# Stick attention two key blocks at a time, projections of 384 columns, and tile 6's expert lists during the last queries

## The chip, the core and the metric

The kernel runs on one core of a Trainium2 chip, in one launch. The metric is the device time of that launch in microseconds. The core's engines are TensorE (PE; its weight loads stand apart as PEld), VectorE (DVE), ScalarE (ACT), GpSimd (POOL) and SyncE (SP), beside 16 DMA engines. Engines run their own queues in order and wait for each other through semaphores.

## The reference

One decoder block on 1024 tokens of width 1024, all in 32-bit floats. A normalised input feeds three token mixers; their results are gated, summed, projected and added to x. Then every token chooses 8 x 16 of 16384 experts.

```python
h = rms_norm(x, g_mix)
# A: stick-breaking attention, 8 heads of 64, strictly causal
z = q k^T * 64**-0.5
log_keep = where(past, log_sigmoid(-z), 0)
between = reverse_cumsum(log_keep) - log_keep
a = where(past, exp(log_sigmoid(z) + between), 0);  y_sb = a v
# B: 12 heads of 64 in 3 groups, window 128 keys at stride 1, 4, 16, rms_norm on q and k, merged by lse
# C: 4 heads of 128 over 256 memory tokens, rms_norm on q and k, softmax
x = x + (sum of sigmoid(h W_gate + b) * (y_* W_o)) W_out
h2 = rms_norm(x, g_ffn)
sc = (h2 w_q) . subkeys                 # 8 heads x 2 halves x 128 scores a token
s1, i1 = top_k(sc[0], 16); s2, i2 = top_k(sc[1], 16)
top_s, pos = top_k(s1[:, None] + s2[None, :], 16);  gate = softmax(top_s)
out = x + sum over 8 x 16 of gate * gelu(u[idx] . h2) * v[idx]
```

## The kernel before

Tokens lie in 8 tiles of 128, taken in three groups: tiles 0 and 1, then 2 to 4, then 5 to 7 (`GROUPS = (2, 3, 3)`; below: the first, second and third group). `phase1` takes a group through stages: `stick_breaking` (four pairs of heads), `dilated` with the pieces of `memory_attn` set in between, `gating`, `out_proj`, `ffn_norm`, and `select`, the queries and scores of the experts. The keys and values of the first two groups are kept in DRAM for the later ones.

Matmul operands are in 32-bit floats: a product shows as two PE records. A projection `proj_T` works with at most 256 columns (`SUB = 2` tiles), so a group of three tiles is taken as 256 + 128 columns, each with its own PSUM bank (tile name `bank`, four buffers) and, for normalised q and k, its own chain in `head_norm` and `rstd_rows`: ScalarE squares, a product with ones, VectorE's ms, ScalarE's Ln, Exp and Square, and three or four VectorE passes. `Pipe` delays each piece's later parts by one tick, so that they stand behind the next piece's first products.

In `stick_part` a round takes one key block b against one or two query tiles: scores z in a bank, Abs, Exp and Ln on ScalarE (tile `e`), sp on VectorE, and one tick later (part1) the product with `ntri` (the sum inside the block) and with `nones` over S (the sum of later blocks), Exp, and S += sp; another tick later (part2) the product with v. A double tile works on 2 heads x 256 columns, the third tile of a group alone on 2 x 128.

Six tiles have their experts gathered: for every step, 128 rows of u and 128 of v come by one indirect DMA each, issued by GpSimd (L1030); VectorE multiplies u with h2 and sums (L1092, two passes a step), Gelu on ScalarE once in four steps, and TensorE sums v by weights (L1116; pb at L1083 spreads h2). There are 768 steps. Tiles 4 and 6 (`DENSE`) are computed against all experts instead: `gate_matrix` turns their lists into a matrix (tiles `ab`, products into g, stored to gd), and `dense` streams u and v once (L1134), adding up in acc (L1264).

The lists come from VectorE: `top16` (L819 to L823) for 16 halves, `pairs` and another `top16` for 8 heads. For a group's first tile they are made in `select` (the part `first`); for the others in `topk`, which is a side job, in the order 1st, 3rd, 2nd tile.

What stands beside what is decided in the main loop: a step is issued, then `fill` takes pieces of the rest (phase 1, gate matrix, dense) by the planner's costs, until a due time.

```python
            due = max(due + LEAST, pe - LEAST)
            while filler[0] is not None and (dma > pe or pe < due):
                a, b = fill(1)
```

What is left of the steps when the rest is done runs alone at the end (the tail). A scheduler then orders each engine's queue; ScalarE keeps the program's order.

Of the kernel before, what the change touches and what calls it, by code (L numbers as in the profile page):

```python
# [17 lines left out]
D = 1024  # L18
# [28 lines left out]
SUB = 2  # L47
# [29 lines left out]
def block_kernel(ctx: ExitStack, tc: tile.TileContext, io):  # L77
# [239 lines left out]
    def rstd_rows(ssq, n, dim):  # L317

        y = tmp.tile([128, NS], F32, name="rs")
        ms = tmp.tile([128, NS], F32, name="ms")  # L320
        nc.vector.tensor_scalar(ms[:, :n], ssq, 1.0 / dim, EPS, op0=OP.mult, op1=OP.add)
        actf(y[:, :n], ssq, AF.Ln, scale=1.0 / dim, bias=eps)
        actf(y[:, :n], y[:, :n], AF.Exp, scale=-0.5)
        a = tmp.tile([128, NS], F32, name="sq")
        actf(a[:, :n], y[:, :n], AF.Square)
        nc.vector.scalar_tensor_tensor(a[:, :n], a[:, :n], -0.5, ms[:, :n], op0=OP.mult, op1=OP.mult)
        nc.vector.scalar_tensor_tensor(y[:, :n], a[:, :n], 1.5, y[:, :n], op0=OP.add, op1=OP.mult)
        return y

    def norm_T(xT, n, gain, out):  # L330

        ps_ = []
        for c0 in range(0, n, NS):
            w = min(NS, n - c0)
            p = bank()
            for k in range(KD):
                sq = tmp.tile([128, NS], F32, name="sq")
                actf(sq[:, :w], xT[:, k, c0:c0 + w], AF.Square)
                mm(p[:, :w], ones, sq[:, :w], start=k == 0, stop=k == KD - 1)
            ps_.append((c0, w, p))  # L340
        yield
        for c0, w, p in ps_:
            y = rstd_rows(p[:, :w], w, D)
            for k in range(KD):
                nc.vector.scalar_tensor_tensor(out[:, k, c0:c0 + w], xT[:, k, c0:c0 + w], gain[:, k:k + 1],
                                               y[:, :w], op0=OP.mult, op1=OP.mult)
        yield

    def proj_T(w, h, n, c0=0):

        p = bank()
        if type(w) is tuple:
            wh, wl = w
            for k in range(KD):
                hh, hl = (x[:, k % 4, c0:c0 + n] for x in h[1][k // 4])
# [4 lines left out]
        for piece, o, m in pieces(h[0], c0, n):  # L360
# [4 lines left out]
    def pieces(h, c0, n):  # L365

        if type(h) is not list:
            return [(h[:, :, c0:c0 + n], 0, n)]
# [12 lines left out]
    def head_norm(p, n, dim, lhs, done):  # L381

        sq = tmp.tile([128, NS], F32, name="sq")
# [41 lines left out]
    def stick_breaking(pipe, weights, hT, n0, G, oT):  # L425
        N = G * 128
        t0 = n0 * 128
        for p in range(4):
# [7 lines left out]
            w = weights("w_in", p)  # L436
            for i, g in subs(G):
                pq = proj_T(w, hT, g * 128, i * 128)
                for s in range(2):
                    r = slice(64 * s, 64 * s + 64)  # L440
                    nc.vector.tensor_scalar(q[r, s, i * 128:(i + g) * 128], pq[r, :g * 128], 0.125, None, op0=OP.mult)
                pipe.tick()
                yield
            w = weights("w_in", 4 + p)
            for i, g in subs(G):
                pk = proj_T(w, hT, g * 128, i * 128)
                actf(kT[:, t0 + i * 128:t0 + (i + g) * 128], pk[:, :g * 128], AF.Copy)
                pipe.tick()
                yield
# [10 lines left out]
    def stick_part(pipe, p, kT, v, q, n0, G, out):  # L460
# [49 lines left out]
    def dilated(pipe, weights, hT, n0, G, oT, between):  # L510
        N = G * 128
        t0 = n0 * 128
        for pp in range(2):
            ks, vs, b0s = [], [], []
            for g, (dil, nb) in enumerate(DIL):
# [18 lines left out]
                wq = weights("w_in", NB_SB + pr)  # L534
                for i0, m in subs(G):
                    c = slice(i0 * 128, (i0 + m) * 128)
                    pq = proj_T(wq, hT, m * 128, i0 * 128)

                    def done_q(y, pq=pq, g=g, c=c, m=m * 128):
                        for s in range(2):  # L540
                            r = slice(64 * s, 64 * s + 64)
                            nc.vector.scalar_tensor_tensor(qpad[r, 2 * g + s, c], pq[r, :m], gs[r, 0:1],
                                                           y[r, :m], op0=OP.mult, op1=OP.mult)
                    part = head_norm(pq, m * 128, 64, ones64, done_q)
                    pipe.tick()
                    pipe.push(part)
                    yield
                wk = weights("w_in", NB_SB + 6 + pr)
                for i0, m in subs(G):
                    c = slice(w0 + i0 * 128, w0 + (i0 + m) * 128)  # L550
                    pk = proj_T(wk, hT, m * 128, i0 * 128)

                    def done_k(y, pk=pk, k=k, w0=w0, pr=pr, c=c, m=m * 128, last=i0 + m == G):
                        nc.vector.scalar_tensor_tensor(k[:, c], pk[:, :m], gk_dil, y[:, :m],
                                                       op0=OP.mult, op1=OP.mult)
                        if last and n0 + G < NT:
                            nc.scalar.dma_start(c_dk[pr, :, t0:t0 + N], k[:, w0:w0 + N])
# [830 lines left out]
```

## Time and profile before

| | |
|---|---|
| three runs | 4009.22, 4027.1 (median), 4034.66 us |
| profiled execution | 4013.32 us, span 4011.5 us, mean granted TensorE clock 0.905 |
| busy | PE 3361.7, DVE 2632.8, POOL 1506.7, ACT 1256.0 us |
| moved | 1186.65 MB, mean 296 GB/s |
| first step at | 506.9 us |
| last dense addition | 3930 us |

Busy time is the union of an engine's instructions. PEclk is the TensorE clock that was granted, as a share of full speed. "DMA share" is the mean busy share of the 16 DMA engines. In a row of a timeline stand the start, the time, the engine, the line, the operation and the tiles (out<-in), and in brackets the idle time before it with what ended it. In a row of waits stand who waited for whom, the total, the times and the longest. In a row of groups: the count, the busy time, the mean in ns, and the idle time before.

### The profile page before, as it was taken

The page shows a single profiled execution, that of the slowest core. Times are in us where ns is not written, and L with a number is a line of the kernel's source. Part 1 is how long each engine was busy: PE and PEld are TensorE (multiplying, and loading weights), DVE is VectorE, ACT ScalarE, POOL GpSimd, SP SyncE. Part 2 cuts the span into 40 slices and gives each one's busy share as a digit, 9 for nine tenths or more (in the row PEclk, how much of TensorE's full clock was granted, in tenths as well). Part 3 has the DMA queues.
Part 4 walks back from the last instruction along what each step waited for, and adds up shares of the span by engine and source line. Part 5 has one row for each costly group of instructions (what it writes and reads, how often), then busy time and mean ns, then how long its engine had stood idle before and what let it go on. Part 6 is the DMA issues. An engine that isn't in the chain of part 4 may idle for free.

```text
span 4011.5 us, 65667 instructions
## 1 busy us (share of the span) xinstructions
PE 3361.7 (84%) x24130; PEld 2529.9 (63%) x24130; DVE 2632.8 (66%) x8339; ACT 1256.0 (31%) x2637; POOL 1506.7 (38%) x1544
## 2 busy tenths in 40 slices
PE   7999788878799888878878999793366999999995
PEld 6889666656555676655756556681134888878772
DVE  5443885455434557876555466469886888888885
ACT  4442343433300113544434211110023444433340
POOL 0000043433345443444434344355552343333335
PEclk9999888988899998998989999895587999999996
DMA  4345487877699997787877799897998899999989
GB/s 148 110 129 176 152 306 245 293 268 264 234 330 385 374 352 285 268 280 257 317 254 270 268 381 379 331 364 278 353 329 313 331 375 356 364 359 360 348 307 340
DMA packets 347034, 1186.65 MB, mean 296 GB/s; under 512 B 38808, under 2 KB 80792, under 8 KB 327256
## 3 DMA queue, kind: packets, MB, share of 16 engines
q0 software_dynamic: 221184, 805.40, 54.9%
q1 hardware_dynamic: 102960, 338.34, 23.3%
q10 hardware_dynamic: 22568, 38.70, 2.6%
q8 instruction: 191, 3.13, 0.3%
q14 instruction: 131, 1.07, 0.1%
HBM read 1142.58 MB, written 39.71 MB: 295 GB/s over the span
## 4 chain that ended last, share of the span: by engine, by line
PE 62%; DVE 16%; issue 6%; DMA 5%; another core or an unknown queue 5%; ACT 5%; POOL 1%; ACTq 1%; SPq 0%; DVEq 0%; POOLq 0%
PE bank L116 34%; PE bank L1134 18%; PE po L1116 7%; DVE u L1092 5%; ACT e L127 2%; DMA u<-in_u,iT 1%; PE pb L1083 1%; DMA gd<-g 1%; PE bank L120 1%; ACT L125 1%; DMA v<-in_v,iT 1%; DVE ab L1159 1%; DVE ul L1219 1%; POOL v L1030 1%
## 5 line engine op out<-in xcount | busy, mean ns | idle before, releaser
L1030 POOL DMA_INDIRECT u<-in_u,iT x768 | 759.5, 989 | 1778.2 <-DVE u L1092 757.5
L1092 DVE SCALAR_TENSOR_TENSOR u<-u,pb 128x512 f32<-128x512 f32 x1536 | 1009.2, 680 | 216.9 <-PE pb L1083 105.3
L1030 POOL DMA_INDIRECT v<-in_v,iT x768 | 746.4, 972 | 716.5 <-PE po L1116 490.6
L116 PE MATMUL bank<-wide,w 128*128 128x128 f32 (+2 forms) x2304 | 554.9, 397 | 34.3 <-ACT S L127 16.0
L1116 PE MATMUL po<-v,wz 128*32 128x256 f32 x6144 | 466.7, 416 | 85.6 <-DVE wz L1105 34.0
L116 PEld LDWEIGHTS bank<-wide,w 128*128 128x128 f32 x2304 | 396.8, 201 | 179.5 <-issue 21.9
L1116 PEld LDWEIGHTS po<-v,wz 128*32 128x32 f32 x6144 | 187.5, 115 | 318.1 <-issue 109.0
L1134 PE MATMUL bank<-hh,uh 128*128 128x256 f32 x1024 | 293.4, 286 | 32.2 <-issue 31.8
L116 PE MATMUL bank<-w,wide 128*128 128x128 f32 x2304 | 279.4, 280 | 29.2 <-issue 15.7
L1134 PE MATMUL bank<-hh,ul 128*128 128x256 f32 x1024 | 293.2, 286 | 5.8 <-DVE ul L1219 5.0
L116 PEld LDWEIGHTS bank<-w,wide 128*128 128x128 f32 x2304 | 269.2, 195 | 45.4 <-issue 24.8
L1134 PE MATMUL bank<-hl,uh 128*128 128x256 f32 x1024 | 291.1, 284 | 0.0
L127 ACT ACTIVATE e<-bank 128x256 f32<-128x256 f32 (+2 forms) x256 | 117.2, 458 | 502.0 <-PE bank L116 202.3
L1083 PE MATMUL pb<-b,which 96*128 96x512 bf16 x384 | 141.3, 419 | 102.6 <-DVE u L1092 83.1
L1134 PEld LDWEIGHTS bank<-hh,uh 128*128 128x128 f32 x1024 | 197.8, 193 | 38.7 <-issue 34.6
L1134 PE MATMUL bank<-vh,wh 128*128 128x512 f32 x512 | 212.2, 419 | 7.8 <-ACT wh L127 5.7
L1134 PEld LDWEIGHTS bank<-hh,ul 128*128 128x128 f32 x1024 | 197.6, 193 | 15.2 <-issue 7.3
L1134 PE MATMUL bank<-vl,wh 128*128 128x512 f32 x512 | 200.7, 392 | 0.0
L1134 PE MATMUL bank<-vh,wl 128*128 128x512 f32 x512 | 198.5, 392 | 0.6 <-DVE wl L1251 0.6
L1134 PEld LDWEIGHTS bank<-hl,uh 128*128 128x128 f32 x1024 | 197.7, 193 | 0.4 <-issue 0.4
L1264 DVE TENSOR_TENSOR acc<-acc,bank 128x512 f32<-128x512 f32 x256 | 168.8, 685 | 37.2 <-PE bank L1134 31.7
L116 PE MATMUL bank<-big,w 128*128 128x128 f32 (+1 forms) x1024 | 182.6, 335 | 3.1 <-issue 3.1
(259 smaller groups left out, 6117.1 us busy)
## 6 DMA issues: line engine op xcount, KB each, us to landing
vr<-in_vd SPq DMA_DIRECT2D x64, 1024.0 KB
ur<-in_uT SPq DMA_DIRECT2D x64, 1024.0 KB
w<-in_w_in SPq DMA_DIRECT2D x102, 512.0 KB
w<-in_w_gate SPq DMA_DIRECT2D x72, 512.0 KB
w<-in_w_pq SPq DMA_DIRECT2D x48, 512.0 KB
g<-gd SPq DMA_DIRECT2D x16, 1024.0 KB
w<-in_w_o SPq DMA_DIRECT2D x48, 256.0 KB
w<-in_w_out SPq DMA_DIRECT2D x24, 512.0 KB
```

Of the source, the lines that this page charges most:

```text
L116: nc.tensor.matmul(out, lhsT, rhs, **kw)
L120: nc.tensor.transpose(out, in_, ident)
L125: nc.scalar.preload_act_table_set(s)
L127: nc.scalar.activation(out, in_, f, **kw)
L1030: nc.gpsimd.indirect_dma_start(out=t, out_offset=None, in_=io[kind], in_offset=bass.IndirectOffsetOnAxis(ap=ap, axis=0))
L1083: nc.tensor.matmul(pb, which[:, jj].rearrange("p q s -> p (q s)"), box["b3"][:, hh * 512:(hh + 1) * 512], start=True, stop=True)
L1092: nc.vector.scalar_tensor_tensor(u[:, f], u[:, f], 1.0, pb, op0=OP.mult, op1=OP.mult, accum_out=self.parts[:, hh, i:i + 1])
L1116: nc.tensor.matmul(po[32 * k:32 * k + 32, h:h + 256], wz[:, i, :], v[:, 256 * k:256 * k + 256], start=jj == 0 and i == 0, stop=jj == QB - ...
L1134: nc.tensor.matmul(out, lhsT, rhs, **kw)
L1159: nc.vector.tensor_scalar(ab[:, 0, :], iota, sl[:, 0, t:t + 1], sl[:, 2, t:t + 1], op0=OP.is_equal, op1=OP.mult)
L1219: nc.vector.tensor_sub(lo, r[:, x], hi)
L1264: nc.vector.tensor_add(acc[:, i, f], acc[:, i, f], o)
```

## The change

1. `stick_single` takes a single tile two key blocks at a time: z, e and sp hold 2 blocks x 2 heads x 128. The nearer block's sum is added to the farther one by a product of its own (`nones`, sp). 
2. `proj_T` takes all of a group's columns (384) into one bank; q, k and memory queries have one norm chain for the group. `rstd_rows` scales the sum in the bank, and Ln reads it there. `memory_attn` works by head, with the parts of both sub-tiles in one step.
3. In the third group `select` makes the lists of tiles 5 and 6; tile 6's lie in three tiles of `ab`. `topk` runs in the order 1st, 2nd, 3rd tile.
4. `dense` loads and splits its first operands ahead of the wait for the gate matrix.

```diff
     def rstd_rows(ssq, n, dim):
-        nc.vector.tensor_scalar(ms[:, :n], ssq, 1.0 / dim, EPS, op0=OP.mult, op1=OP.add)
-        actf(y[:, :n], ssq, AF.Ln, scale=1.0 / dim, bias=eps)
+        nc.vector.tensor_scalar(ssq, ssq, 1.0 / dim, EPS, op0=OP.mult, op1=OP.add)
+        actf(y[:, :n], ssq, AF.Ln)
...
             for i, g in subs(G):
-                yield from stick_part(pipe, p, kT, v, q[:, :, i * 128:(i + g) * 128], n0 + i, g,
-                                      oT[:, p, i * 128:(i + g) * 128])
+                args = pipe, kT, v, q[:, :, i * 128:(i + g) * 128], n0 + i, oT[:, p, i * 128:(i + g) * 128]
+                yield from stick_single(*args) if g == 1 else stick_part(*args[:5], g, args[5])
+    def stick_single(pipe, kT, v, q, n, out):
+        S = tmp.tile([128, 2, NS], F32, name="S", bufs=1)[:, :, :128]
+        for b in range(n, -1, -2):
+            bs = [b, b - 1][:b + 1]
+            m = len(bs)
+            z = bank().rearrange("p (x s n) -> p x s n", x=2, s=2)
+            for x, y in enumerate(bs):
+                for s in range(2):
+                    mm(z[:, x, s], kT[:, y * 128:(y + 1) * 128], q[:, s], start=x == 0 and s == 0, stop=False,
+                       skip_group_check=True)
...
+            actf(e[:, :m], z[:, :m], AF.Abs)
+            actf(e[:, :m], e[:, :m], AF.Exp, scale=-1.0)
+            actf(e[:, :m], e[:, :m], AF.Ln, bias=1.0)
+            nc.vector.scalar_tensor_tensor(sp[:, :m], z[:, :m], 0.0, e[:, :m], op0=OP.max, op1=OP.add)
+            def part1(b=b, m=m, z=z, e=e, sp=sp):
+                for x in range(m):
+                    mm(z[:, x], ntri, sp[:, x], start=False, stop=False, skip_group_check=True)
+                    if b < n:
+                        mm(z[:, x], nones, S, start=False, stop=False, skip_group_check=True)
+                if m == 2:
+                    mm(z[:, 1], nones, sp[:, 0], start=False, stop=True, skip_group_check=True)
+                actf(e[:, :m], z[:, :m], AF.Exp)
...
-                wq = weights("w_in", NB_SB + pr)
-                for i0, m in subs(G):
-                    pq = proj_T(wq, hT, m * 128, i0 * 128)
-                    part = head_norm(pq, m * 128, 64, ones64, done_q)
+                pq = proj_T(weights("w_in", NB_SB + pr), hT, N)
+                part = head_norm(pq, N, 64, ones64, done_q)
...
-            for _ in range(2 * len(subs(G))):
+            for _ in range(2):
                 next(between)
...
         scs = [wide.tile([128, 8 * NMAX], F32, name="wide")[:, :2048].rearrange("p (a b) -> p a b", a=16)
-               if i == SUB else sc.tile([128, 16, 128], F32, name="sc") for i in range(G)]
+               if G > SUB and i == 1 else sc.tile([128, 16, 128], F32, name="sc") for i in range(G)]
+        lists = [new_lists()]
+        if n0 + G == NT:
+            a, b, c = (gm.tile([128, 2, 128], F32, name="ab") for _ in range(3))
...
             def first(hp=hp):
-                top16(s16[:, h, hp % 2, :], i16[:, h, hp % 2, :], scs[0][:, hp, :])
+                for l, x in zip(lists, scs):
+                    half_list(hp, x, *l)
...
-        for i in (0, 2, 1)[:G] if G > SUB else range(G):
+        for i in range(G):
...
         while len(stored) < ND:
             cost[0] += 1500
             yield
-        while next(gates) < ND:
-            cost[0] += 800
-            yield
         hh = dp.tile([128, KD, TD], F32R, name="hh", bufs=1)
...
         us[0] = split(ur[0], 0, "u", 2)
+        while next(gates) < ND:
+            cost[0] += 800
+            yield
```

Three places in the built order show what moves; line numbers of the changed kernel differ by up to 45. First TensorE, in the stick attention of tile 7 (single): before, two rounds of one key block, with a step's products (po) between them. e,big is the product with v, qpad,big the scores of a later block.

```order
L116 MATMUL bank<-e,big 64x128 x2
L116 MATMUL bank<-sp,ntri 128x128
L116 MATMUL bank<-S,none 128x128
L116 MATMUL bank<-sp,ntri 128x128
L116 MATMUL bank<-S,none 128x128
L1116 MATMUL po<-v,wz 32x256 x11
L116 MATMUL bank<-qpad,big 128x128 x2
L116 MATMUL bank<-e,big 64x128 x2
L116 MATMUL bank<-sp,ntri 128x128
L116 MATMUL bank<-S,none 128x128
```

In the changed order the same place holds one round of two blocks:

```order
L116 MATMUL bank<-qpad,big 128x128 x4
L116 MATMUL bank<-e,big 64x128 x4
L116 MATMUL bank<-sp,ntri 128x256
L116 MATMUL bank<-S,none 128x256
L116 MATMUL bank<-sp,ntri 128x256
L116 MATMUL bank<-S,none 128x256
L116 MATMUL bank<-sp,none 128x256
```

Products are twice as wide, with one more (sp,none), and TensorE meets ScalarE's e and VectorE's sp once where it met them twice.

Second VectorE, in the third group's last queries: before, the list of tile 5 alone (scores in sc, values in s, the 8 heads' merges in ts and pos).

```order
L819 MAX ts<-sc 128x8
L819 MAX s_20802<-sc 128x8
L820 MAX_INDEX pos<-ts,sc 128x8
L820 MAX_INDEX i_20803<-s_20802,sc 128x8
L821 MATCH_REPLACE sc<-ts,sc 128x112
L821 MATCH_REPLACE sc<-s_20802,sc 128x128
```

In the changed order tile 6's (scores in wide, lists in ab) stands beside it:

```order
L859 MAX s_19472<-sc 128x8
L859 MAX ab<-wide 128x8
L860 MAX_INDEX i_19473<-s_19472,sc 128x8
L860 MAX_INDEX ab<-ab,wide 128x8
L861 MATCH_REPLACE sc<-s_19472,sc 128x128
L861 MATCH_REPLACE wide<-ab,wide 128x128
L862 MAX s_19472<-sc 128x8
L862 MAX ab<-wide 128x8
L863 MAX_INDEX i_19473<-s_19472,sc 128x8
L863 MAX_INDEX ab<-ab,wide 128x8
L1137 SCALAR_TENSOR_TENSOR u,parts<-u,pb 128x512 x4
```

Each score row of the queries now brings ten passes where it brought five, ahead of the steps' products (the last row).

Third SyncE's loads at the start of dense: sl is tile 6's list for the gate matrix, g the finished matrix, ur and vr the experts' rows. Before:

```order
L1149 DMA sl<-seld 128x384
L1008 DMA b_24146<-b3d 96x1024
L1077 DMA row<-xres 32x256 x4
L247 DMA g<-gd 128x8x256 x2
L247 DMA ur<-in_uT 128x2048 x3
```

In the changed order:

```order
L247 DMA ur<-in_uT 128x2048
L1194 DMA sl<-seld 128x384
L247 DMA ur<-in_uT 128x2048
L247 DMA vr<-in_vd 128x2048 x2
L1053 DMA b_23144<-b3d 96x1024
L1122 DMA row<-xres 32x256 x4
L247 DMA g<-gd 128x8x256 x2
```

The first u rows move from behind g to ahead of sl. By the counts of steps (rows of L1092, in the changed kernel L1137, on VectorE), 601.5 steps stand ahead of the first dense addition before and 556.5 now, and behind the last one 28 before and 70 now.

More of the change, by code (lines that the diff above doesn't have):

```diff
@@ L330, in norm_T, with proj_T @@
     def norm_T(xT, n, gain, out):
[L332 to L340, printed above, removed]
-        yield
[L342 to L346, printed above, removed]
+        p = bank()
+        for k in range(KD):
+            sq = tmp.tile([128, NMAX], F32, name="sq")
+            actf(sq[:, :n], xT[:, k, :n], AF.Square)
+            mm(p[:, :n], ones, sq[:, :n], start=k == 0, stop=k == KD - 1)
+        yield
+        y = rstd_rows(p[:, :n], n, D)
+        for k in range(KD):
+            nc.vector.scalar_tensor_tensor(out[:, k, :n], xT[:, k, :n], gain[:, k:k + 1], y[:, :n],
+                                           op0=OP.mult, op1=OP.mult)
         yield
-    def proj_T(w, h, n, c0=0):
+    def proj_T(w, h, n):
         p = bank()
@@ L548, in dilated @@
[L548 to L557, printed above, removed]
-                    part = head_norm(pk, m * 128, 64, ones64, done_k)
-                    pipe.tick()
-                    pipe.push(part)
-                    yield
+                pq = proj_T(weights("w_in", NB_SB + pr), hT, N)
@@ new lines, in done_q @@
+                def done_q(y, pq=pq, g=g):
+                    for s in range(2):
+                        r = slice(64 * s, 64 * s + 64)
+                        nc.vector.scalar_tensor_tensor(qpad[r, 2 * g + s, :N], pq[r, :N], gs[r, 0:1],
+                                                       y[r, :N], op0=OP.mult, op1=OP.mult)
+                part = head_norm(pq, N, 64, ones64, done_q)
+                pipe.tick()
+                pipe.push(part)
+                yield
+                pk = proj_T(weights("w_in", NB_SB + 6 + pr), hT, N)
@@ new lines, in done_k @@
+                def done_k(y, pk=pk, k=k, w0=w0, pr=pr):
+                    nc.vector.scalar_tensor_tensor(k[:, w0:w0 + N], pk[:, :N], gk_dil, y[:, :N],
+                                                   op0=OP.mult, op1=OP.mult)
+                    if n0 + G < NT:
+                        nc.scalar.dma_start(c_dk[pr, :, t0:t0 + N], k[:, w0:w0 + N])
+                part = head_norm(pk, N, 64, ones64, done_k)
+                pipe.tick()
+                pipe.push(part)
+                yield
@@ L730, in back @@
             actf(oT[:, 6 + h, i0 * 128:i0 * 128 + N], pt[:, :N], AF.Copy)
-        part = head_norm(pq, N, 128, ones, done)
-        pipe.tick()
-        pipe.push(part, scores, mix, mix2, back)
+        return box, scores, mix, mix2, back
     def gating(pipe, weights, hT, N, oT, mT):
@@ L859, in select, with new_lists, half_list @@
         pipe.flush()
[L860 removed]
+        side.append(topk(n0, G, scs, out, lists))
+    def new_lists():
+        return (tk.tile([128, 8, 2, 16], F32, name="s16", bufs=2), tk.tile([128, 8, 2, 16], U32, name="i16"),
+                tk.tile([128, 8, 16], F32, name="ts"), tk.tile([128, 8, 16], U32, name="pos"))
+    def half_list(hp, scores, s16, i16, ts, pos):
+        h = hp // 2
+        top16(s16[:, h, hp % 2, :], i16[:, h, hp % 2, :], scores[:, hp, :])
+        if hp % 2:
+            cand = candidates(scores)
+            pairs(cand, s16, h)
+            top16(ts[:, h, :], pos[:, h, :], cand[:, h, :])
     def candidates(sc):
```

141 lines of the change are left out of this document (73 added, 68 removed).

## The prediction

> **What bounds the kernel now.** I read the page first: which engine the chain that ended last runs through.
>
> ```profile
> PE 3361.7 (84%) x24130; PEld 2529.9 (63%) x24130; DVE 2632.8 (66%) x8339; ACT 1256.0 (31%) x2637; POOL 1506.7 (38%) x1544
> PE 62%; DVE 16%; issue 6%; DMA 5%; another core or an unknown queue 5%; ACT 5%; POOL 1%; ACTq 1%; SPq 0%; DVEq 0%; POOLq 0%
> ```
>
> TensorE carries 62% of the chain, but an 84% average over stages with different limits prices nothing. So the second view is the table of busy times by stretch. I found the borders in the timeline, by the shapes and weights that each stage uses: stick attention of the second group (514 to 760), its dilated and memory attention (to 1102), gating (to 1314); the same two stages of the third group (1563, 1919 to 2243), its last queries (2597 to 2719), the stretch to the first dense product (3036), dense, and the tail.
>
> ```profile
> core 0: us, PE busy (x) PEld busy (x) DVE busy (x) ACT busy (x) POOL busy (x), PEclk, DMA share, GB/s
> 514.00:760.00 246.00, 203.90 (x1487) 151.62 (x1485) 152.65 (x566) 102.30 (x192) 108.02 (x114) 0.90 0.79 280
> 760.00:1102.00 342.00, 272.08 (x2121) 201.33 (x2122) 177.61 (x603) 124.94 (x284) 129.35 (x137) 0.88 0.74 262
> 1102.00:1314.00 212.00, 207.88 (x1059) 115.67 (x1061) 92.18 (x295) 15.40 (x41) 105.55 (x113) 1.00 0.96 358
> ...
> 1563.00:1919.00 356.00, 293.79 (x2190) 212.53 (x2189) 264.50 (x1018) 169.35 (x313) 153.80 (x159) 0.91 0.75 260
> 1919.00:2243.00 324.00, 267.50 (x2263) 197.32 (x2262) 181.22 (x602) 127.91 (x290) 131.50 (x140) 0.90 0.80 277
> ...
> 2597.00:2719.00 122.00, 112.75 (x852) 91.11 (x852) 81.66 (x392) 18.80 (x74) 65.84 (x70) 0.96 0.93 345
> 2719.00:2908.00 189.00, 67.14 (x567) 21.43 (x567) 167.67 (x749) 10.90 (x24) 99.81 (x101) 0.55 0.87 317
> 2908.00:3036.00 128.00, 84.52 (x566) 47.96 (x559) 105.03 (x423) 37.44 (x136) 67.56 (x71) 0.84 0.92 333
> 3036.00:3930.00 894.00, 846.17 (x5845) 693.75 (x5845) 747.76 (x1468) 348.89 (x551) 323.81 (x295) 0.98 0.92 344
> 3930.00:4011.50 81.50, 38.92 (x269) 8.06 (x268) 40.57 (x135) 1.44 (x7) 46.55 (x50) 0.53 0.92 356
> ```
>
> Four regimes. In both attention stages nothing is full: TensorE busy 79 to 83%, granted clock 0.88 to 0.91, DMA share 0.74 to 0.80; waits between engines set the pace. Gating and dense are TensorE at full clock, with DMA nearly full as well. From 2719 to 3036 VectorE is the bound (89%, then 82%) and TensorE's clock falls to 0.55. The tail holds expert steps alone and is bound by their fetches.
>
> **The change, term by term.** The sum starts from the profiled execution's 4013.3 us, which lies 13.8 under the median of the three runs.
>
> *Pairs of key blocks.* The single tiles' four stretches in the third group are 1612.3:1642.4, 1698.9:1730.6, 1792.5:1829.1, 1885.8:1918.7, and in the second 544.4:561.8, 603.4:625.7, 671.0:697.5, 738.5:760.6; the double tiles' stretches stand before each. Their sums, in the order single third, single second, double third, double second:
>
> ```profile
> sum 131.30, PE 107.64 PEld 77.97 DVE 96.95 ACT 70.53 POOL 59.41; mean PE 26.91 PEld 19.49 DVE 24.24 ACT 17.63 POOL 14.85
> sum 88.30, PE 72.74 PEld 53.26 DVE 53.35 ACT 45.27 POOL 32.08; mean PE 18.19 PEld 13.32 DVE 13.34 ACT 11.32 POOL 8.02
> sum 146.10, PE 112.83 PEld 73.29 DVE 100.48 ACT 86.81 POOL 59.74; mean PE 28.21 PEld 18.32 DVE 25.12 ACT 21.70 POOL 14.94
> sum 78.00, PE 62.57 PEld 41.06 DVE 51.12 ACT 45.80 POOL 36.39; mean PE 15.64 PEld 10.26 DVE 12.78 ACT 11.45 POOL 9.10
> ```
>
> Single tiles make 4x8 = 32 rounds in the third group, 4.1 us each, and 20 in the second, 4.4 us each. Where that goes shows on TensorE in one of them:
>
> ```profile
> 1803.63 0.71 PE L116 MATMUL bank<-qpad,big 128*128 128x128 f32 x4
> 1806.48 0.44 PE L116 MATMUL bank<-e,big 128*64 128x128 f32 x4 [2.14 <-issue]
> ...
> 1807.18 0.39 PE L116 MATMUL bank<-S,none 128*128 128x128 f32 x2
> 1807.40 0.39 PE L116 MATMUL bank<-sp,ntri 128*128 128x128 f32 x2
> ...
> 1810.66 0.44 PE L116 MATMUL bank<-e,big 128*64 128x128 f32 x4 [1.99 <-ACT e L127]
> ```
>
> Each round ends in about 2 us of waiting for ScalarE's four passes over e. A round of two key blocks has the shapes of a double tile's round (512 elements on ScalarE and VectorE), and those take 146.1/28 = 5.2 and 78.0/16 = 4.9 us. To it I add one more 256-column product (1807.18 to 1807.40 is 0.22 for 128 columns, so 0.44) and 0.3 of a step more per round, some 0.4: 6.0 and 5.7 us. That is 16 x 6.0 = 96 for the third group, and 8 x 5.7 + 4 half-filled rounds at 4.4 = 63 for the second: **60 us less**. Bounds: 25 if only half the waits go, 85 if a round runs at a double tile's bare 5.2 and 4.9.
>
> *Projections of 384 columns, memory attention by head.* The product itself costs the same per column. What goes is banks: a dilated unit took nine of the four rotating PSUM banks (two each for q, k and their two norms, one for v), and takes five. What TensorE waited for there, in 760:1102 and then in 1919:2243:
>
> ```profile
> PE bank L116 <- DVE qpad L542: 9.8, 4, 6.2
> PE bank L116 <- ACT S L127: 7.5, 2, 6.0
> PE bank L116 <- ACT sq L127: 4.7, 3, 2.5
> PE bank L116 <- ACT rs L127: 3.8, 2, 3.1
> ...
> PE bank L116 <- ACT S L127: 11.3, 4, 7.0
> PE bank L116 <- DVE qpad L542: 6.8, 6, 1.7
> ```
>
> The qpad, sq and rs rows (25.1) belong to the split norms; S (18.8) is memory attention, of which I count half. **35 us less**, bounds 0 (others come last instead) and 70 (the clock comes back from 0.88 as well).
>
> The norm's new wait costs nothing: Ln now reads what VectorE writes back to the bank, but it waited for VectorE's ms already.
>
> ```profile
> 799.05 0.47 ACT L127 ACTIVATE rs<-bank,eps 128x256 f32<-128x256 f32 x1 [0.23 <-DVE ms L321]
> ```
>
> *Tile 6's lists in the last queries.* One list is 16 rounds of five passes like the first row below (22), eight merges of five (10.5) and the sums of pairs (3.4): 36 us of VectorE.
>
> ```profile
> L823 DVE FIND_INDEX8 i<-s,sc 128x8 uint32<-128x128 f32 x16 | 4.5, 285 | 0.0
> ...
> 3035.17 0.68 DVE L1092 SCALAR_TENSOR_TENSOR u<-u,pb 128x512 f32<-128x512 f32 x1
> 3035.78 0.08 DVE L1092 DVE_READ_ACCUMULATOR u<-u,pb 128x1 f32 x1
> ...
> L1092 DVE SCALAR_TENSOR_TENSOR u<-u,pb 128x512 f32<-128x512 f32 x172 | 110.8, 677 | 0.2 <-DMA u<-in_u,iT 0.2
> 3067.97 0.55 PE L1134 MATMUL bank<-hh,uh 128*128 128x256 f32 x1 [28.64 <-issue]
> ...
> 3035.05 1.03 ACTq L1177 DMA_DIRECT2D gd<-g  x2
> 3035.75 11.97 DMA gd<-g
> 3075.89 0.40 PE L1134 MATMUL bank<-vh,wh 128*128 128x512 f32 x1
> ```
>
> In the last queries VectorE goes from 82 to 118 of 122 us, in front of the step products that TensorE's pb and po wait for. I count **12 us more**; bounds 0 and 36 (the whole list uncovered).
>
> *From the last query to the first dense product.* Counted over VectorE's rows, 601.5 steps stand before the first dense addition now and 556.5 in the changed order: 45 fewer. A step occupies VectorE for two passes at a pitch of 0.61 (3035.17 to 3035.78) and some 0.1 of small ones, 1.3 us: 45 x 1.3 = 59, plus the list, 36. Since VectorE bounds this stretch, 95 us go. Then, TensorE sat idle 28.6 us before its first dense product because the ur load stood on SP behind two g loads that waited for the gate matrix; the new SP order has ur, vr and the split halves ahead of the matrix. What is late next is g itself. Its last store took 12 us (3035.75); with an estimated 8 for the load, that is 20 us after the store's issue, where now 41 pass (3035.05 to 3075.89) to the first product that needs it: some 20 us more. **115 us less**; bounds 140 (all idle of the stretch goes too) and 60 (the steps alone).
>
> *The tail.* Steps that are not issued before dense must come after it, since dense holds 144 steps before and 146 after: behind the last dense addition stand 28 steps now and 70 in the changed order. In 3940:3990, with nothing beside them:
>
> ```profile
> L1092 DVE SCALAR_TENSOR_TENSOR u<-u,pb 128x512 f32<-128x512 f32 x37 | 23.7, 684 | 21.1 <-DMA u<-in_u,iT 8.5 <-issue 8.5 <-remote 4.0
> L1030 POOL DMA_INDIRECT u<-in_u,iT x17 | 15.9, 936 | 5.6 <-issue 3.7 <-DVE u L1092 1.0 <-DMA v<-in_v,iT 0.6
> ```
>
> 18.5 steps in 50 us, 2.70 each: 42 x 2.70 = **113 us more** (107 to 118). So the early start of dense is nearly paid back.
>
> Beside this stands a rule that speaks against more VectorE work close to the fetches. In the matrix stretch, 2908:3036, where VectorE runs back-to-back tensor-scalar passes, a fetch's issue took:
>
> ```profile
> L1030 POOL DMA_INDIRECT u<-in_u,iT x36 | 34.9, 969 | 56.4 <-DVE u L1092 24.1 <-DVE acts L1100 13.0 <-DVE ab L1161 10.2
> ```
>
> That is 969 ns against 936 in the tail. The Trainium skill, page "SBUF — State Buffer", section "SBUF: two separate sides", says that GpSimd cannot write DMA descriptors while VectorE runs a two-port pass, and puts such a DMA at about 3100 ns instead of 620. By that the 68 fetches of the new matrix stretch would cost up to 170 us; by the rows, 68 x 33 ns, about 2. The trace does not agree with the large figure here, and I count nothing.
>
> **Sum:** 4013 - 60 - 35 + 12 - 115 + 113 = 3928 us. Against the median of runs I add half of the 13.8: **3935**.
>
> **The rivals.**
>
> *Only an exchange.* The steps' fetches set the pace of the attention stages, so faster chains only wait longer, and dense's earlier start goes into the tail: 4013 + 12 - 115 + 113 = 4023, within 1%. For it: DMA share 0.74 to 0.80, and the count of steps by stage hardly changes. Against it: gating moves 358 GB/s where these stages move 260 to 280, and the waits named are for e and qpad, not for transfers.
>
> *Pairs alone.* The wide projections only move their waits (35 becomes 0), and the early dense start gains just what the tail costs: 4013 - 60 + 12 = 3965. This is also the case in which that part of the change doesn't do what it says.
>
> *Slower: VectorE takes over before dense.* In 2719:2908 VectorE at 89% pushed TensorE's granted clock to 0.55. If the second list does this to the last queries, their TensorE work (112.8 us at 0.96) takes 197 us, +75 instead of +12; and if the matrix stretch, now with a list in it, is held as well, it gives only 40 of the 115. From the forecast that is +63 + 75: 4066. It decides only once it takes more than the 85 us that the forecast gains. For it: 118 of 122. Against it: in 2719:2908 TensorE had little of its own to do, and here it has a full queue. The Trainium skill, page "TensorE: Matmul & The Clock Gate", section "What's actually happening", has the clock at half after an idle window of about 3.4 us; the trace agrees (0.50 to 0.55 where TensorE waits long).
>
> **How the numbers follow.** Forecast 0.60, pairs alone 0.14, exchange 0.18, slower 0.08. All bounds taken together give 3825 to 4082; the four cases with their spread hold 8 in 10 between 3850 and 4025. About 1% (40 us) is what a measurement of this kernel can tell from no change. The first two cases are faster by more than that, with a small part of the second within it and of the third beyond it: faster 0.72, same 0.20, slower 0.08.
>
> **What would show it.** Single-tile rounds of two blocks at 5.5 to 6.5 us; the qpad wait mostly gone from the dilated stages; last queries 125 to 145 us with a clock over 0.9; the first dense product some 200 to 220 us after the last query, without the 28 us of idle before it; the tail near 195 us at 2.7 us a step. I am wrong if the attention stages keep their 246, 342, 356 and 324 us, if the clock falls in the last queries, or if dense itself grows past 894.

## The result, and the profile after

| | kernel before | changed kernel |
|---|---|---|
| runs | 4005.49 to 4034.66 us, median 4018.16 (4) | 3905.36 to 3922.7 us, median 3917.27 (4) |
| ratio | | 0.9743, 95% interval 0.9695 to 0.979 |
| profiled execution | 4013.32 us, span 4011.5 | 3922.7 us, span 3920.9 |

The change saves 101 us by the medians, 91 by the two spans. The page of the changed kernel, its busy times, and then the table by stretch, cut at the same places of the program: both attention stages of the second group and its gating, the same three of the third, the last queries, two pieces up to the first dense product, dense, the tail.

```profile
PE 3328.7 (85%) x23106; PEld 2416.8 (62%) x23106; DVE 2606.2 (66%) x8133; ACT 1210.0 (31%) x2385; POOL 1517.0 (39%) x1544
```

```profile
core 0: us, PE busy (x) PEld busy (x) DVE busy (x) ACT busy (x) POOL busy (x), PEclk, DMA share, GB/s
506.30:742.70 236.40, 195.17 (x1320) 134.98 (x1320) 143.43 (x526) 97.11 (x158) 104.80 (x110) 0.91 0.80 285
742.70:1026.80 284.10, 246.97 (x1831) 156.04 (x1830) 161.72 (x520) 110.57 (x219) 126.82 (x135) 0.92 0.86 304
1026.80:1238.90 212.10, 211.01 (x1071) 119.15 (x1070) 101.34 (x321) 15.44 (x41) 111.20 (x118) 1.00 1.00 381
...
1479.20:1808.40 329.20, 283.92 (x1965) 191.71 (x1966) 250.13 (x962) 157.32 (x243) 152.65 (x157) 0.92 0.79 277
1808.40:2121.50 313.10, 268.79 (x1989) 166.42 (x1988) 173.39 (x547) 115.35 (x229) 129.09 (x137) 0.87 0.80 282
2121.50:2383.30 261.80, 248.78 (x1380) 154.95 (x1378) 154.46 (x556) 44.45 (x154) 122.18 (x129) 0.98 0.97 364
...
2481.50:2615.70 134.20, 112.21 (x850) 92.02 (x851) 105.68 (x584) 19.16 (x75) 64.87 (x69) 0.95 0.89 316
2615.70:2671.20 55.50, 12.59 (x137) 4.67 (x136) 50.69 (x180) 5.37 (x8) 20.84 (x19) 0.53 0.65 223
2671.20:2830.00 158.80, 94.97 (x592) 61.18 (x596) 139.07 (x584) 42.84 (x140) 62.58 (x65) 0.66 0.79 282
...
2900.00:3720.00 820.00, 798.94 (x5555) 653.26 (x5554) 702.76 (x1387) 324.34 (x514) 318.12 (x283) 1.00 0.93 350
3720.00:3921.00 201.00, 94.44 (x607) 21.89 (x607) 97.88 (x329) 3.69 (x18) 122.51 (x130) 0.52 0.95 355
```

The four attention stretches go from 246, 342, 356 and 324 us to 236, 284, 329 and 313: 106 us in all. The last queries grow by 12. From the last query to the first dense product it is 217 us instead of 349. Dense itself (first product with vh to last addition) stays: 854 and 856.5 us. The tail grows from 81 to 208 us, with 70 steps behind the last addition in place of 28. So the end of the program gains nothing on balance (+12 -116 +2 +127 = +25), and the saving stands in the attention stages, with some 10 us in small stages. Tile 6's lists in the last queries and the early start of dense are called the end part below.

### The profile page after: what moved, and what is told of

It is laid out like the page before. It is cut to its first block, busy times and chain, and to the rows that moved or that the text cites. A ratio compares the mean times of both kernels' runs of the same rounds, so it can differ in the third digit from the quotient of the medians.

```text
span 3920.9 us, 62997 instructions
## 1 busy us (share of the span) xinstructions
PE 3328.7 (85%) x23106; PEld 2416.8 (62%) x23106; DVE 2606.2 (66%) x8133; ACT 1210.0 (31%) x2385; POOL 1517.0 (39%) x1544
## 5 line engine op out<-in xcount | busy, mean ns | idle before, releaser
L1137 DVE SCALAR_TENSOR_TENSOR u<-u,pb 128x512 f32<-128x512 f32 x1536 | 1006.3, 682 | 281.9 <-PE pb L1128 91.0
L1161 PE MATMUL po<-v,wz 128*32 128x256 f32 x6144 | 476.8, 424 | 140.2 <-DVE wz L1150 76.7
L116 PE MATMUL bank<-wide,w 128*128 128x384 f32 x1536 | 524.6, 495 | 7.0 <-issue 4.3
L116 PEld LDWEIGHTS bank<-wide,w 128*128 128x128 f32 x1536 | 291.5, 193 | 213.9 <-issue 23.5
L127 ACT ACTIVATE e<-bank 128x512 f32<-128x512 f32 (+2 forms) x208 | 109.5, 527 | 478.0 <-PE bank L116 190.1
L1179 PE MATMUL bank<-u 128*128 128x256 f32 x544 | 163.6, 301 | 24.1 <-ACT u L127 21.5
```

Of the source, the lines that this page charges most:

```text
L116: nc.tensor.matmul(out, lhsT, rhs, **kw)
L127: nc.scalar.activation(out, in_, f, **kw)
L1137: nc.vector.scalar_tensor_tensor(u[:, f], u[:, f], 1.0, pb, op0=OP.mult, op1=OP.mult, accum_out=self.parts[:, hh, i:i + 1])
L1161: nc.tensor.matmul(po[32 * k:32 * k + 32, h:h + 256], wz[:, i, :], v[:, 256 * k:256 * k + 256], start=jj == 0 and i == 0, stop=jj == QB - ...
L1179: nc.tensor.matmul(out, lhsT, rhs, **kw)
```

## The experiments

Every ratio below is against the kernel before on the same chip, since chips differ: the kernel before takes 4007 to 4018 us on some ("4010 chips", the prediction's among them) and 3707 to 3713 on others ("3710 chips"). Ratios of the two kinds are not mixed.

**The changed kernel on a 3710 chip** (no edit).

> The changed kernel itself, beside the kernel before, on the chip that gets this job. Theory (the end part, that is tile 6's lists in the last queries and the early start of dense, is an exchange against the tail): pairs and wide projections alone gave 0.988 on a chip where the kernel before takes 3713 us; the end part adds some 4 us in the last queries, takes 115 us from the stretch before dense and adds 42 steps of 2.75 us = 115 us to the tail. So 0.986 to 0.992 if the kernel before takes about 3710 us here, and 0.970 to 0.979 if it takes about 4020. Rival (the end part is a gain of its own of 50 us or more): 0.970 to 0.977 also where the kernel before takes 3710 us.

0.986 (0.9841 to 0.9879): 3653.71 against 3707.13 us, a gain of 53 us where the prediction's chip gave 101. That is the lower end of the theory's 0.986 to 0.992, and the rival falls. As the program is the same to the instruction, this trace also shows what the two kinds of chips differ in. In order of time, the second group's gating and the third group's stick attention, dilated and memory attention, and gating:

```profile
954.40:1165.20 210.80, 210.80 (x1071) 119.43 (x1070) 103.12 (x325) 15.46 (x41) 111.79 (x119) 1.00 1.00 387
1406.50:1675.80 269.30, 261.18 (x1965) 178.69 (x1965) 247.67 (x960) 156.65 (x242) 151.55 (x157) 0.99 0.92 339
1675.80:1936.90 261.10, 245.26 (x1989) 154.11 (x1990) 172.41 (x544) 114.95 (x229) 128.56 (x137) 0.95 0.92 334
1936.90:2180.40 243.50, 242.72 (x1380) 151.47 (x1379) 154.44 (x559) 43.95 (x154) 121.51 (x129) 1.00 1.00 384
```

Against the rows above: stick attention 269 for 329, dilated 261 for 313, the third group's gating 244 for 262, the second group's 211 for 212. VectorE's busy time in the stick attention is nearly the same (247.67 and 250.13), so its operations are not slower; what differs is TensorE's granted clock and the waits. What TensorE waited for in the third group's stick attention, on the first chip and then here:

```profile
PE bank L116 <- ACT e L127: 17.9, 9, 6.3
PE bank L116 <- issue: 17.2, 20, 5.2
PE bank L116 <- DVE sp L520: 7.1, 2, 5.8
```

```profile
PE bank L116 <- DVE sp L520: 2.4, 2, 1.2
...
PE bank L116 <- ACT e L127: 1.2, 3, 0.5
```

On the first chip the engines pause for up to 5 or 6 us at a time, "issue" among the causes (nothing that the profile shows), and TensorE's granted clock is 0.92 in place of 0.99. Up to the first step (at 501 and 502 us) the two traces agree within 1.5 us, so the pauses appear only once steps run. The four attention stretches make up 185 of the 270 us between the spans; the tail differs too (189 and 208 us).

The traces tell where many of these pauses start. In the 5.8 us that the last row of the first chip puts down to sp, TensorE, ScalarE and VectorE show this:

```profile
1658.39 0.38 PE L1128 MATMUL pb<-b,which 96*128 96x512 bf16 x1
...
1661.54 0.38 ACT L127 ACTIVATE e<-bank 128x256 f32<-128x256 f32 x1 [9.79 <-remote]
1661.61 0.69 DVE L1137 SCALAR_TENSOR_TENSOR u<-u,pb 128x512 f32<-128x512 f32 x1 [2.38 <-remote]
...
1664.61 1.22 PE L116 MATMUL bank<-sp,ntri 128*128 128x128 f32 x4 [5.84 <-DVE sp L520]
```

ScalarE waits there for the scores in the bank and VectorE for pb, both products of TensorE, whose last record ends at 1658.8. Both start 2.8 us after that end, and sp, which TensorE waits for next, is late because they are. "Remote" (on the page "another core or an unknown queue") is what the profile writes where a wait ends and no record of this core ended shortly before it. By the semaphores in this trace, 114 of its 115 such waits are for TensorE, and the first comes at 516 us. All six traces of 4010 chips have them (ScalarE alone waits 177 to 338 us in this way), and none of the eight of 3710 chips has one. The chain of the changed kernel on the 3710 chip has no such share, where that of the kernel before, shown with the prediction, has 5%:

```profile
PE 69%; DVE 14%; DMA 11%; ACT 2%; issue 2%; POOL 1%; ACTq 1%; SPq 0%; POOLq 0%; DVEq 0%
```

So a part of the waits for e and sp on the first chip is not the chain of ScalarE and VectorE, but TensorE's own products that are late to release them. Why they are late, and whether it is the chip or what else ran on it, no run here shows.

**The kernel before once more, for its trace** (no edit).

> The kernel before itself, for its trace on a chip where it takes about 3710 us. Theory (on the chip of the prediction's trace the engines pause in the attention stages once steps run beside them, and here they do not): stick attention of the second and third group 200 and 280 us (247 and 356 on the first chip), dilated and memory attention 280 and 280 (341 and 325), while gating (212 and 257) and dense (854) stay within 6%; TensorE's waits for e in the third group's stick attention fall from 37 us to under 8. Rival (transfers are slower on the first chip): gating and dense, which move the most bytes a second, are 8% shorter or more here as well.

The run came to a 4010 chip (4017.55 us), so it does not decide between the two by itself. The changed kernel's two traces speak for the theory: gating and dense are 1 to 7% shorter on the 3710 chip (dense 837 for 856.5 us), the attention stages 12 to 18%, and the waits for e nearly go. This run shows that the long attention stages are no oddity of one chip:

```profile
509.10:749.90 240.80, 201.11 (x1488) 150.09 (x1486) 151.60 (x560) 102.61 (x194) 108.12 (x114) 0.91 0.81 287
749.90:1099.30 349.40, 280.54 (x2121) 210.90 (x2122) 177.62 (x603) 125.14 (x284) 129.18 (x137) 0.83 0.72 255
...
1559.90:1916.40 356.50, 289.69 (x2188) 211.03 (x2188) 264.79 (x1019) 168.93 (x312) 152.97 (x159) 0.92 0.75 259
1916.40:2242.90 326.50, 268.70 (x2266) 198.39 (x2267) 181.10 (x604) 128.15 (x290) 131.63 (x140) 0.90 0.79 275
```

**Pairs alone, wide projections alone, both without the end part** (all on one 3710 chip; both once more on a 4010 chip). Pairs alone is the kernel before with `stick_single`; wide alone is the changed kernel without it and without the end part:

```diff
-                yield from stick_single(*args) if g == 1 else stick_part(*args[:5], g, args[5])
+                yield from stick_part(*args[:5], g, args[5])
```

The end part is undone by taking tile 6's lists out of `select`, with the old order in `topk` and the wait for the gate matrix first:

```diff
-        if n0 + G == NT:
-            a, b, c = (gm.tile([128, 2, 128], F32, name="ab") for _ in range(3))
...
-        for i in range(G):
+        for i in (0, 2, 1)[:G] if G > SUB else range(G):
...
+        while next(gates) < ND:
+            cost[0] += 800
+            yield
         hh = dp.tile([128, KD, TD], F32R, name="hh", bufs=1)
```

> The kernel before with stick_single alone. Read from the two profiles (single-tile stretches 24 us shorter in all): 20 to 30 us faster than before, 0.993 to 0.995. Rival, the forecast's 60 us (the profiles' borders between stages hide part of it): 0.985.

> The kernel before with the projections of 384 columns and the memory parts by head alone. Read from the two profiles (dilated and memory stages 69 us shorter, q and k projections of the stick stage up to 20): 70 to 90 us faster, 0.978 to 0.983. Rival, the forecast's 35 us: 0.991.

> Pairs and wide projections, with tile 6's list, the order of lists and the start of dense as before: 601.5 steps ahead of the first dense addition and 28.5 behind the last. If the early start of dense is more than paid back by the tail (+12, -116, +127 by the profiles), this is 10 to 30 us faster than the changed kernel: 0.967 to 0.972 of before. Rival: the early start is where the gain came from, and this is slower than the changed kernel, 0.98 or more.

> Pairs and wide projections without the end part once more, for the price of the end part where the kernel before takes some 4010 us. Theory (the end part is an exchange on both kinds of chips; on the first it cost 12 in the last queries and 127 in the tail for 116 before dense): 0.966 to 0.976 where the kernel before takes about 4010 us, the same as the changed kernel's 0.974 within 10 us or up to 25 us better; 0.986 to 0.990 where it takes about 3710. Rival (the end part is the larger half of the gain where the kernel before is slow): 0.985 or more there.

| | chip | ratio (interval) | us |
|---|---|---|---|
| pairs alone | 3710 | 0.9964 (0.995 to 0.9978) | -15 |
| wide alone | 3710 | 0.9939 (0.9926 to 0.9953) | -25 |
| both, no end part | 3710 | 0.9881 (0.9866 to 0.9895) | -47 |
| changed kernel | 3710 | 0.986 (0.9841 to 0.9879) | -53 |
| both, no end part | 4010 | 0.9699 (0.9669 to 0.9729) | -113 |
| changed kernel | 4010 | 0.9743 (0.9695 to 0.979) | -101 |

The first three expectations were worked out from the prediction's chip. Pairs alone stay below what either theory gave them; wide alone comes nearer to the rival, the forecast's 35 us, than to the theory; both together miss their range on the 3710 chip and meet it on the 4010 one. The number of their rival (0.98 or more) does come on the 3710 chip, but not its reason: the changed kernel is no more than 6 us faster there. The two parts nearly add up (15 + 25 = 40 of 47). On both kinds of chips the intervals with and without the end part overlap: at this planner's rate it is an exchange, as the run on the 4010 chip was to show. And pairs bring little there, for a reason that stands in the sums over the single tiles' stretches of the third group, wide alone and then both:

```profile
sum 117.30, PE 107.61 PEld 73.45 DVE 104.90 ACT 69.09 POOL 62.15; mean PE 26.90 PEld 18.36 DVE 26.23 ACT 17.27 POOL 15.54
```

```profile
sum 96.50, PE 95.97 PEld 64.60 DVE 85.28 ACT 56.97 POOL 55.01; mean PE 23.99 PEld 16.15 DVE 21.32 ACT 14.24 POOL 13.75
```

With pairs TensorE is busy 95.97 of 96.50 us: 16 rounds of 6.0 us, all of it work. Without them only 9.7 us were idle to begin with. The rest of the 21 us is largely work that stands elsewhere now: the double tiles' stretches grew from 111 to 118 us and the projections between them from 51 to 56. Over the whole stick attention of the third group TensorE's busy time hardly changes (263.6 and 261.3 us), and the stage gets 8.4 us shorter (278.7 to 270.3).

**One list in the last queries, and the load order.** Both start from the changed kernel; the first takes the `lists.append` of tile 6 out, the second puts the wait for the gate matrix ahead of `hh` again (the three lines above).

> The changed kernel without tile 6's lists in the last queries (topk makes them, in the new order of tiles; dense's loads stay ahead of the wait for the gate matrix). In the built order 574.5 steps stand before the first dense addition (556.5 with the lists) and 52 behind the last one (70). Theory: the last queries get 4 to 12 us shorter, the stretch before dense 36 us of list and 18 x 1.3 = 23 us of steps longer, the tail 18 x 2.75 = 50 us shorter: within 10 us of the changed kernel. Rival (VectorE's list in the stretch is what the change gains): 35 us or more slower than the changed kernel.

> The changed kernel with the wait for the gate matrix put back ahead of dense's first loads. 565 steps stand before the first dense addition (556.5 in the changed kernel), 70 behind the last one. Theory: TensorE stands idle some 28 us before its first dense product again, and 8.5 steps of 1.3 us stand ahead of it in place of steps inside dense: 15 to 30 us slower than the changed kernel. Rival (the idle time is filled by other work, since fetches and steps go on meanwhile): within 7 us of it.

One list: 3654.55 us (0.9865, 0.9846 to 0.9884) beside the changed kernel's 3653.71. From the last query to the first product with vh it takes 280.5 us for 231.2, and the tail 139.5 for 189.1: -1 (the last queries) +49 -50. The theory's sum holds, and the rival falls; but the last queries got 1 us shorter, not 4 to 12. Load order: 3666.39 us (0.9892, 0.9872 to 0.9912), 12.7 us more, between the two expectations. TensorE's first dense product there:

```profile
2634.18 0.55 PE L1179 MATMUL bank<-hh,uh 128*128 128x256 f32 x1 [20.93 <-ACT uh L127]
```

It comes 32 us later than in the changed kernel (2602.4), but the first product with vh only 17 later (2642.4 for 2625.6): in the changed kernel g is late instead. And dense, with 8.5 steps fewer in it, is 6 us shorter (831 for 837).

**More steps inside dense.** What the tail takes is set by the planner's rate for dense, `BW[1]`: the GB/s of transfers that it reckons with when it decides how many steps stand there. First both parts without the end part at 400, then the changed kernel at 380, 400 and 430:

```diff
-BW = 295.0, 360.0
+BW = 295.0, 430.0
```

> Pairs and wide projections without the end part, with the planner's rate of transfer in dense set from 360 to 400: 609 steps stand before the first dense addition, 159 in dense, none behind the last one (601.5, 138 and 28.5 at 360). The changed kernel at 400 took 0.966 of the kernel before. Theory (what costs is a tail in which TensorE does nothing for dense; the end part only decides how many steps stand on which side): the tail of 28.5 steps goes, some 78 us, and dense's 144 to 159 steps cost TensorE 20 us more: 0.970 to 0.976. Rival (dense cannot take more steps than it does, its length grows by the steps' fetches): 0.985 to 0.990, as at 360.

> The changed kernel with the planner's bandwidth for dense at 400 instead of 360: 18 steps instead of 70 behind the last dense addition. A step costs 3.0 us in the tail. If dense is bound by TensorE, the 52 steps cost it some 0.75 us each and the kernel gains 60 to 115 us over the changed one (0.945 to 0.96 of before). Rival: the DMA engines are full beside dense at 350 GB/s already, the 52 steps lengthen dense by 3 us each, and the time stays within 15 us of the changed kernel's.

> The changed kernel with the planner's rate of transfer in dense at 380 in place of 360: 559.5 steps before the first dense addition, 44 behind the last one (556.5 and 70 in the changed kernel, 563 and 18 at 400). Theory (a step in the tail costs 2.7 us and inside dense, while the transfers keep up, nearly nothing): linear between 0.986 at 360 and 0.966 at 400, so 0.974 to 0.979. Rival (the gain comes at the end alone, when the tail is nearly gone): 0.982 or more.

> The changed kernel with that rate at 430: 565.5 steps before the first dense addition, none behind the last. Theory (at 400 dense already moves 390 to 406 GB/s, and no stretch of any run moved more, so further steps inside dense wait for transfers and lengthen it by what the tail loses): 0.962 to 0.970, as at 400. Rival (the 18 steps of the tail, 50 us, go as well): 0.950 to 0.956.

| | chip | ratio (interval) | dense, tail us |
|---|---|---|---|
| both, no end part, 360 | 3710 | 0.9881 (0.9866 to 0.9895) | 836, 83 |
| both, no end part, 400 | 3710 | 0.979 (0.977 to 0.981) | 862, 4 |
| changed, 360 | 3710 | 0.986 (0.9841 to 0.9879) | 837, 189 |
| changed, 400 | 3710 | 0.9659 (0.9641 to 0.9678) | 887, 55 |
| changed, 360 | 4010 | 0.9743 (0.9695 to 0.979) | 856, 208 |
| changed, 380 | 4010 | 0.9677 (0.9635 to 0.972) | 900, 133 |
| changed, 430 | 4010 | 0.9513 (0.9474 to 0.9551) | 951, 4 |

A step in the tail takes 208/70 = 3.0 us on the 4010 chip. From 380 to 430 the tail loses 44 steps: 38 of them go into dense, which grows by 51 us, 1.3 us each, and 6 into the stretch before it (tail -129). At 400 on the 3710 chip dense takes 45.5 steps more for 50 us, 1.1 each, and not the 0.75 of the expectation. That expectation held in its gain, 0.020 of the kernel before or some 75 us, where 60 to 115 was named; its ratio of 0.945 to 0.96 was worked out from the prediction's chip. Its rival falls.

The expectations for 380 and 430 name ratios of a 3710 chip, and these runs came to a 4010 one, so they are read by their differences from 360. At 380 the ratio fell by 0.0066, just short of the 0.007 to 0.012 expected and above the rival's 0.004 (tail -75, dense +43); the intervals at 360 and 380 overlap. At 430 it fell by 0.023, which lies in the theory's 0.016 to 0.024 and not in the rival's 0.030 to 0.036. But the theory's reason (dense is full of transfers and lengthens by what the tail loses) does not fit: from 380 on, dense lengthens by 40% of that. As no run at 400 came to a 4010 chip, the step from 400 to 430 itself is not measured. Dense at 430, and the last 107 us, after the last fetch:

```profile
2820.00:3700.00 880.00, 811.66 (x5817) 642.49 (x5814) 751.44 (x1666) 312.00 (x512) 445.15 (x409) 0.98 1.02 400
3700.00:3807.00 107.00, 98.32 (x631) 82.54 (x630) 75.14 (x125) 39.97 (x62) 7.32 (x7) 0.95 0.51 193
```

It moves 400 GB/s for 880 us at a clock of 0.98. That the rate has a limit near 406 still stands, since no piece of 100 or 200 us that was read moved more in either run; but at 430 dense holds it longer, and all steps fit. Without the end part the step from 360 to 400 brings 38 us: the tail loses 79, dense grows by 26, and the stretch before dense by 15, since 7.5 more steps stand there. That part the expectation had left out, and 0.979 lies above its 0.970 to 0.976, though below the rival's 0.985.

So the best version on a 4010 chip is the changed kernel at 430 (3810.15 us against 4008.07), and on a 3710 chip the one at 400. There the end part pays: 0.9659 with it, 0.979 without. Dense and the tail take 76 us more with it, but the stretch before dense takes 123 less (244 for 367). Whether it pays at 430 too was not run.

## Why the prediction came out, point by point

The time was forecast at 3935 and came to 3917, but three terms were mis-sized, and their errors cancel: pairs gave 36 us less than forecast, wide projections 53 more, and the tail took 14 more.

**What bounds the kernel:** right. The attention stages, read as paced by waits, gave the gain; gating and dense, read as full, hardly moved (257 to 262 us in the third group, 854 to 856.5). What the reading left out is that a part of these waits is TensorE's own late products, which only 4010 chips show.

**Pairs, 60 less (bounds 25 to 85): mis-sized.** The single tiles' stretches fell from 131.3 and 88.3 us to these, third and second group:

```profile
sum 117.60, PE 101.99 PEld 66.61 DVE 81.86 ACT 57.26 POOL 49.75; mean PE 25.50 PEld 16.65 DVE 20.46 ACT 14.31 POOL 12.44
sum 77.60, PE 70.20 PEld 45.99 DVE 49.69 ACT 39.57 POOL 33.24; mean PE 17.55 PEld 11.50 DVE 12.42 ACT 9.89 POOL 8.31
```

That is 24 us, just below the lower bound: 7.35 us a round in the third group for the 6.0 forecast, and in the second 6.5 on the mean of all 12 rounds, for 63/12 = 5.25. The failed step is "16 x 6.0 = 96": against the 131.3 it takes 35 us out of a stretch in which, by its own quoted row, TensorE was idle for only 131.3 - 107.6 = 23.7. Its work does not go away with the waits. Of the idle time 15.6 us stay, so 8 went; the other 6 are TensorE's work, 3.6 of it the steps' products (po and pb), which stand in other stretches now. And of the two waits of 2 us that the forecast quotes from one round, only one is put down to ScalarE's e; the other is "issue". On the 3710 chip the round did take 6.0, but the round that it replaced was shorter there too.

**Wide projections, 35 less (0 to 70): mis-sized.** The dilated and memory stages lost 57 and 11 us, the projections in stick attention 6 and 13: 88. The failed step is "the product itself costs the same per column". TensorE's projection products in the second group's dilated stage, before and after:

```profile
L116 PE MATMUL bank<-wide,w 128*128 128x128 f32 (+2 forms) x512 | 105.8, 366 | 13.4 <-ACT S L127 7.5 <-DVE qpad L542 2.6 <-issue 1.7
```

```profile
L116 PE MATMUL bank<-wide,w 128*128 128x384 f32 x256 | 88.2, 497 | 0.0
```

Nearly the same columns in half the products take 17.6 us less, and their 13.4 us of idle time go to nothing. Not all of the 17.6 is the columns': on one 3710 chip the narrow products (pairs alone, the same stage) take 10 us less than here, and the wide ones no less (89.0 us, wide alone):

```profile
L116 PE MATMUL bank<-wide,w 128*128 128x128 f32 (+2 forms) x512 | 95.5, 342 | 3.1 <-ACT S L127 2.6 <-DVE qpad L591 0.5
```

So 6.5 us come with the width on the 3710 chip too, and the other 11 appear only on the first chip, which has the pauses and the lower clock in this stage (0.87 before the change, 0.95 here). Of the stage's 57 us, busy TensorE makes up 25 and idle time 32: I had counted only the second. The forecast's reason for its own part, banks, held: the qpad wait is gone, and S falls from 18.8 to 3.4 us in the two stages. The size belongs to the 4010 chips, where a second pair of traces (the kernel before, and both parts without the end part) gives 349 and 280 us for this stage; wide alone was worth 25 us on a 3710 one.

**Tile 6's lists, 12 more:** right on this chip (122.0 to 134.2 us, clock 0.95); on the 3710 chip the list costs the last queries 1 us.

**Last query to first dense product, 115 less:** right: 357 to 241 us up to the first product with vh, and both halves came as forecast. Up to the last store of g it is 221 us for 316, the 95 of the steps and the list. From that store on, 20.0 us pass to the product with vh where 41 passed, 21 less for the 20 forecast (the load of g, for which no row was given, stands in the chain with 10.6 us, and the store before it with 8.2 for the 12):

```profile
2836.65 0.85 ACTq L1222 DMA_DIRECT2D gd<-g  x2
...
2856.60 0.80 PE L1179 MATMUL bank<-vh,wh 128*128 128x512 f32 x1 [9.73 <-ACT wh L127]
```

The first dense product no longer waits for its loads; it stands between two products of the gate matrix:

```profile
2832.30 0.71 PE L116 MATMUL bank<-ab 128*128 128x128 f32 x4
2832.77 0.36 PE L1179 MATMUL bank<-hh,uh 128*128 128x256 f32 x1
```

**The tail, 113 more (107 to 118): too low.** It grew by 127, at 3.0 us a step for the 2.70 taken from 50 us of the tail before. GpSimd's issues there, then in the new matrix stretch, 2671:2830:

```profile
L1075 POOL DMA_INDIRECT v<-in_v,iT x70 | 66.0, 943 | 42.3 <-issue 16.1 <-PE po L1161 10.2 <-remote 7.9
L1075 POOL DMA_INDIRECT u<-in_u,iT x66 | 62.1, 941 | 31.0 <-issue 16.1 <-DVE u L1137 9.6 <-DVE gel L1149 4.4
...
L1075 POOL DMA_INDIRECT u<-in_u,iT x33 | 32.4, 981 | 62.6 <-DVE u L1137 30.5 <-DVE ts L859 11.8 <-DVE sc L960 10.1
```

One issue is as long as before (941 ns). The failed step is the stretch that was read: 3940:3990 moved 394 GB/s, but the whole short tail 356, that is 81.2/28 = 2.9 us a step, and the long one moves 355. On the 3710 chip it is 189/70 = 2.7, at 391 GB/s. The last row is the one on which the port rule was weighed: 981 ns beside VectorE's matrix work, so counting nothing was right. The estimate of 170 us by the Trainium skill, page "SBUF — State Buffer", section "SBUF: two separate sides", did not come; whether VectorE's passes here are of the two-port kind no run shows.

**The sum.** Measured, in its order: -24 -88 +12 -116 +127 = -89 (forecast -85), and 91 by the spans. The double tiles took 7 more and dense 2, and small stages 10 less. That it fits is luck of the signs.

**The rivals.** "Only an exchange" was right on the end part, whose sum I had at +10 and which the runs cannot tell from nothing, and wrong on the attention stages, where faster chains did not only wait longer. "Pairs alone" had the wrong one of the two parts as the one that gives nothing. The slower case did not occur: VectorE took 106 of 134 us in the last queries.

## What to carry to other kernels

Price a fusion by the work that its bounding engine keeps: divide a stretch into busy and idle, since here little beyond the idle part went, and do not count a wider matmul as the same columns at the same price. Work moved out of a stretch comes back elsewhere, here in a tail where TensorE was busy for half of the time at half clock; look for the number that decides where it goes (the planner's rate) before taking the exchange for a result. A gain in waits belongs to the chip that showed them: have the ratio from a second chip.

## What the runs showed of the hardware

- The same program took 3651 and 3921 us (spans) on two chips. VectorE's busy time agrees within 0.1% (2604.0 and 2606.2 us), the second group's gating and the first 500 us within 1%. The larger part of the difference is pauses of a few us in the attention stages, once steps run beside them. Both kinds came up more than once.
- On every 4010 chip, and in no trace of a 3710 chip, engines that wait for TensorE's products start late: in the third group's stick attention 1.8 to 4.8 us after the end of the last TensorE record that signals them. These ends are modelled, but both chips' traces have the same 23106 records. The cause stays open.
- One core held 400 GB/s for 880 us, and 406 in one piece of it (3400:3600). The Trainium skill, page "Perfetto Trace Analysis", section "Roofline", gives 358 GB/s as a core's share when its neighbour reads too, and the 16 DMA engines' sum, about 435, as the bound of one alone; the runs here lie between the two.
- GpSimd's indirect fetch took 941 ns to issue in the tail, and 1120 (u) and 1059 (v) inside dense at 430:

```profile
L1075 POOL DMA_INDIRECT u<-in_u,iT x205 | 229.5, 1120 | 314.2 <-DVE u L1137 249.2 <-issue 29.7 <-DMA v<-in_v,iT 10.9
L1075 POOL DMA_INDIRECT v<-in_v,iT x204 | 216.1, 1059 | 121.3 <-PE po L1161 56.1 <-issue 39.7 <-PE bank L1179 10.8
```
